# Half of the up products' low weight parts made by an adding transfer instead of VectorE

## The chip, the core and the metric

The kernel runs on one core of a Trainium2 chip. The time is the device time of one execution in microseconds; the median of three runs is given, and one more execution was recorded by the hardware profiler. TensorE (PE) multiplies, VectorE (DVE) and ScalarE (ACT) work on elements, GpSimd (POOL) does a few small things, and SyncE (SP) issues the transfers between DRAM and SBUF.

## What is computed

A network of two layers over 256 latent and 256 context positions, width 1024. Each layer is a feed-forward block, a token mixer (a gated linear recurrence, an mLSTM and windowed attention, merged by gates), and a second feed-forward block; all of them are normed, shifted and scaled by a condition. In the last layer the context is no longer needed after the mixer. The change touches the feed-forward blocks:

```
def swiglu(h, w1, w3, w2):
    return (jax.nn.silu(h @ w1) * (h @ w3)) @ w2

xl = xl + 0.5 * ml[:, :, 2] * swiglu(ln_mod(xl, norm_g[l, 0], ml[:, :, 0], ml[:, :, 1]),
                                     ffn_w1[l, 0], ffn_w3[l, 0], ffn_w2[l, 0])
```

`w1` and `w3` are 1024 x 2816, `w2` is 2816 x 1024, all in fp32.

## The kernel before

Latents and context lie side by side as 512 columns, with the width on the partitions in eight tiles `k`. A product is done with three matmuls for each `k` (`mm3`, L264 to L266), since PE works on rounded fp32 (`fp32r`): the high part of the weight by the high part of the input, the high part of the weight by the low part of the input, and the low part of the weight by the high part of the input. The inputs' parts are `hh` and `hl`, the weights' are `whi` and `wlo`.

The weights' parts are made on the chip. `raw_tile` loads 1024 KB of fp32 weights into one of three `raw` buffers (L235 or L240 in the profile, issued by SP). `split_w` then takes 512 columns at a time: ACT copies them to `whi`, which rounds them (L249), and DVE subtracts `whi` from them into `wlo` (L250). Each part takes a slot of SBUF from a list that is used in turn; in the feed-forward blocks 27 slots serve the weights, and while the condition's products run, one of them holds their scrap output `junk`.

The 2816 hidden columns are 22 chunks of 128, done in thirds of 8, 7 and 7. For each chunk, `load13` loads `w1` and `w3` (1024 columns each, so two halves of 512 for each product), `mm3` makes `p1` and `p3` with 2 x 8 x 3 matmuls, and `finish` puts them together (silu on ACT, L640, a product on DVE, L641, and the split into `gh` and `gl`, L283 and L284). After the chunks of a third come the down products `dn` of that third. The first three chunks of a block are made together, in tiles called `up`, while the norm is still being finished (`proj_first`). Tiles `p1` and `p3` both appear as `p` in the profile, where buffer numbers are left out.

There are four feed-forward blocks: (layer 0, first), (layer 0, second), (layer 1, first), and (layer 1, second), the last one over latents alone. In the first three, `filled` is true from the third chunk on: in these DVE also makes the condition's products for later norms (`junk` from `ada` tiles, L390), a few after each chunk, as far as `FEEDS` gives them.

The order of PE's instructions is that of the program. The other engines' instructions are put in order by the scheduler of the framework, from priorities and readiness. Each engine and each queue then runs strictly in its order. In the feed-forward blocks POOL runs the power that makes a norm's scale (`py`, L419), and some memsets of the mixer (`xp`, L763) come early on its queue.

Of the kernel before, what the change touches and what calls it, by code (L numbers as in the profile page):

```python
# [9 lines left out]
F32 = mybir.dt.float32  # L10
# [3 lines left out]
AF = mybir.ActivationFunctionType  # L14
ALU = mybir.AluOpType
# [69 lines left out]
def body(ctx, tc, ins, out):  # L85
    nc = tc.nc
# [9 lines left out]
    def nm(s):  # L96
        uid[0] += 1
        return f"{s}_{uid[0]}"
# [5 lines left out]
    def salloc(name, dt=F32, which=1):  # L104
        i = free[which].pop(0)
        t = sp.tile([P, SLOTW * 2 if dt == BF16 else SLOTW], dt, tag=f"slot{i}", name=nm(name))
        slot_of[id(t)] = (i, t, which)
        return t

    def sfree(*ts):  # L110
        for t in ts:
            i, _, which = slot_of.pop(id(t))
            free[which].append(i)
# [12 lines left out]
    def palloc(name, which=1):  # L126
        i = banks[which].pop(0)
        t = pp.tile([P, T], F32, tag=f"bank{i}", name=nm(name))
        bank_of[id(t)] = (i, t, which)
        return t  # L130

    def pfree(*ts):
        for t in ts:
            i, _, which = bank_of.pop(id(t))
            banks[which].append(i)
# [67 lines left out]
    V = nc.vector  # L203
    S = nc.scalar
# [25 lines left out]
    def raw_tile(src, n):  # L230
        r = wp.tile([P, 2048], F32, tag="raw", name=nm("raw"))
        if len(src.shape) == 3:
            nc.sync.dma_start(r[:, :n].rearrange("p (c f) -> p c f", c=src.shape[1]), src)
        else:
            nc.sync.dma_start(r[:, :n], src)  # L235
        return r
# [3 lines left out]
        nc.sync.dma_start(r, src)  # L240
        return r

    def split_w(r, n):

        w = []
        for a in range(0, n, 512):
            e = min(n - a, 512)
            hi, lo = salloc("whi", F32R, 0), salloc("wlo", F32R, 0)
            S.copy(hi[:, :e], r[:, a:a + e])  # L249
            V.tensor_tensor(lo[:, :e], r[:, a:a + e], hi[:, :e].bitcast(F32), op=ALU.subtract)  # L250
            w.append((hi, lo))
        return w

# [21 lines left out]
    def split_act(src, cols=BOTH, name="y"):  # L275

        hi = salloc(name + "h", F32R)
        lo = salloc(name + "l", F32R)
        split_into(hi, lo, src, cols)
        return hi, lo  # L280
# [44 lines left out]
    def ada_second():  # L325

        ps = palloc("ada")
        for k in range(KD):
            if k % 2 == 0:
                r = raw_tile(ins["ada1"][k // 2], 2 * D)  # L330
            for j in range(4):
                o = k % 2 * D + j * TL
                PE.matmul(ps[32 * j:32 * j + 32, 0:TL], cT[:, k, :], r[:, o:o + TL], start=(k == 0), stop=(k == KD - 1))
            if k % 2 and k < KD - 1:
                yield
        sb = salloc("adasb", which=2)
        S.copy(sb[:, 0:TL], ps[:, 0:TL])
        pfree(ps)

        def turn():  # L340
            ps2 = palloc("ada2")
            for q in range(2):
                PE.transpose(ps2[:, q * P:(q + 1) * P], sb[:, q * P:(q + 1) * P], ident)
            sfree(sb)
            b0 = V_ADAB + 32
            V.tensor_tensor(mods[0][:, 2].rearrange("p (j q) s -> p q j s", q=2),
                            ps2[:, 0:TL].rearrange("p (q j r) -> p q j r", q=2, j=4)[:, :, :, 0:2],
                            vec[:, 0, b0:b0 + 16].rearrange("p (j q s) -> p q j s", q=2, s=2), op=ALU.add)
            pfree(ps2)
            ada_done.add((0, 2))  # L350
        defer(2, turn)
# [188 lines left out]
    def lone_finish(p1, p3):  # L540

        c = small([P, 2], "shc")
        for i, p in enumerate((p1, p3)):
            V.tensor_copy(c[:, i:i + 1], p[:, TL:TL + 1])
        sl, t = salloc("silu", which=2), mp.tile([P, TL], F32, tag="xr", name=nm("xt"), bufs=3)
        V.tensor_tensor(sl[:, LAT], p1[:, LAT], rows[0][:, LAT], op=ALU.mult)
        S.activation(sl[:, LAT], sl[:, LAT], AF.Silu, bias=c[:, 0:1])
        V.tensor_tensor(t, p3[:, LAT], rows[0][:, LAT], op=ALU.mult)
        V.scalar_tensor_tensor(sl[:, LAT], t, c[:, 1:2], sl[:, LAT], op0=ALU.add, op1=ALU.mult)
        pfree(p1, p3)  # L550
        return sl
# [35 lines left out]
            wfree(w)  # L587


    def load13(l, j, m):  # L590
        r = raw_tile(ins["w13"][l, j, m], 2048)
        return [split_w(r[:, :1024], 1024), split_w(r[:, 1024:], 1024)]

    def passes_of(streams, load, use, ahead=None, begin=None):

# [27 lines left out]
    def ffn(l, j, streams, order, after, first, ahead, prep=None):  # L623

        n = 0 if j == 0 else 2
        both = len(streams) == 2
        cols = BOTH if both else LAT
        filled = False
        rate = FEEDS.get((l, j), 0) / 48
        second = ada_second() if l + j == 0 else None  # L630
        for ti, (a, b) in enumerate(THIRDS):
            kk = b - a
            gh, gl = [], []

            def finish(p1, p3, lone=False):
                if lone:
                    sl = lone_finish(p1, p3)
                else:
                    sl = salloc("silu", which=2)
                    S.activation(sl[:, cols], p1[:, cols], AF.Silu)  # L640
                    V.tensor_tensor(sl[:, cols], sl[:, cols], p3[:, cols], op=ALU.mult)  # L641
                    pfree(p1, p3)
                h, lo = split_act(sl, cols, "g")
                gh.append(h)
                gl.append(lo)
                sfree(sl)

            m = a
            if ti == 0:
                ps = [palloc("up", 0) for _ in first]  # L650
                if both:
                    proj_first(first, ps, order, prep)
                else:
                    lone_first(l, n, first, ps)
                for i in range(0, len(first), 2):
                    finish(ps[i], ps[i + 1], not both)
                if not both:
                    sfree(rows.pop(0))
                if j == 0 or l == 0:
                    cond_load()  # L660
                    filled = True
                m = a + len(first) // 2
            while m < b:
                w1, w3 = load13(l, j, m)
                p1, p3 = palloc("p1", 0), palloc("p3", 0)
                mm3(p1, w1, KD, hh, hl, cols)
                mm3(p3, w3, KD, hh, hl, cols)
                wfree(w1)
                wfree(w3)
                finish(p1, p3)  # L670
                if second:
                    next(second, None)
                if filled and m < b - 1:
                    feed(2 * rate)
                tick(2 * pe_us(cols, KD))
                m += 1
            if ti == 0:
                need((l, 3 * n + 2))
                gate_scale(l, n)

            def load2(np_):
                r = raw_tile(ins[f"w2_{ti}"][l, j, np_], 2 * kk * P)
                return [split_w(r[:, q * kk * P:(q + 1) * kk * P], kk * P) for q in range(2)]

            def down(s, o, w, ps=None):
                cc = cols if s is None else STREAMS[s]
                if ps is None:
                    ps = palloc("dn", 0)
                    mm3(ps, w, kk, gh, gl, cc)
                for s2 in streams if s is None else (s,):  # L690
                    x_add(l, n, o, ps, s2)
                    if ti == len(THIRDS) - 1:
                        after(s2, o)
                pfree(ps)
                if filled and s is None and ti < 2:
                    feed(rate)
                tick(pe_us(cc, kk))

            def down_first(ws):

                pss = [palloc("dn", 0) for _ in ws]
                for ks in (range(kk - 1), (kk - 1,)):
                    for ps, w in zip(pss, ws):
                        mm3(ps, w, kk, gh, gl, cols, ks)
                for o, (ps, w) in enumerate(zip(pss, ws)):
                    down(None, o, w, ps)

            if ti == len(THIRDS) - 1:
                passes_of(streams, load2, down, ahead, down_first)
            else:  # L710
                passes_of((None,), load2, down, None, down_first)
            if filled and ti == len(THIRDS) - 1:
                cond_free()
            sfree(*gh, *gl)
# [947 lines left out]
```

## Time and profile before

| what | value |
|---|---|
| median of 3 runs | 2201.46 us (2198.39 to 2201.73) |
| the profiled execution, its time | 2198.09 us |
| the profiled execution, its span | 2196.3 us |
| PE busy | 2160.1 us, 98% |
| DVE busy | 1440.5 us, 66% |
| ACT busy | 1026.0 us, 47% |
| POOL busy | 25.3 us, 1% |
| transfers | 310.26 MB, 40.1% of 16 engines' span |

The span runs from the first to the last instruction of the profile; the execution's time has a little around it. Busy times of engines overlap, so they don't add up to the span. The granted clock is the share of TensorE's full speed that the chip allowed: 0.999 over the span.

### The profile page before, as it was taken

The page shows a single profiled execution, that of the slowest core. Times are in us where ns is not written, and L with a number is a line of the kernel's source. Part 1 is how long each engine was busy: PE and PEld are TensorE (multiplying, and loading weights), DVE is VectorE, ACT ScalarE, POOL GpSimd, SP SyncE. Part 2 cuts the span into 40 slices and gives each one's busy share as a digit, 9 for nine tenths or more (in the row PEclk, how much of TensorE's full clock was granted, in tenths as well). Part 3 has the DMA queues.
Part 4 walks back from the last instruction along what each step waited for, and adds up shares of the span by engine and source line. Part 5 has one row for each costly group of instructions (what it writes and reads, how often), then busy time and mean ns, then how long its engine had stood idle before and what let it go on. Part 6 is the DMA issues. An engine that isn't in the chain of part 4 may idle for free.

```text
span 2196.3 us, 32299 instructions
## 1 busy us (share of the span) xinstructions
PE 2160.1 (98%) x12325; PEld 1840.8 (84%) x12325; DVE 1440.5 (66%) x3029; ACT 1026.0 (47%) x2031; POOL 25.3 (1%) x59
## 2 busy tenths in 40 slices
PE   6999999999999999999999999999999999999999
PEld 5778888977787778998888898888889778999999
DVE  5889634578776645699834378733345888868664
ACT  4322233468576534442232244232234778757553
POOL 0000000000000000000000000000000000000000
PEclk9999999999999999999999999999999999999999
DMA  9666422311122322366622237722222222454652
GB/s 362 240 245 227 161 91 101 112 60 61 67 69 77 125 87 96 135 212 225 228 96 110 89 107 273 242 101 94 91 99 95 68 89 92 152 188 169 232 191 96
DMA packets 73643, 310.26 MB, mean 141 GB/s; under 512 B 6928, under 2 KB 10512, under 8 KB 59024
## 3 DMA queue, kind: packets, MB, share of 16 engines
q1 hardware_dynamic: 73488, 308.19, 40.1%
q8 instruction: 97, 1.59, 0.3%
q14 instruction: 58, 0.48, 0.1%
HBM read 303.97 MB, written 4.19 MB: 140 GB/s over the span
## 4 chain that ended last, share of the span: by engine, by line
PE 89%; DVE 5%; ACT 4%; DMA 1%; issue 1%; POOL 0%; SPq 0%; ACTq 0%; DVEq 0%; POOLq 0%
PE p L264 11%; PE p L265 11%; PE p L266 11%; PE dn L264 6%; PE dn L265 6%; PE dn L266 6%; PE pg L264 3%; PE pg L265 3%; PE pg L266 3%; PE pj L264 2%; PE pj L265 2%; PE pj L266 2%; PE up L264 2%; PE up L266 2%; PE up L265 2%; PE pb L266 1%
## 5 line engine op out<-in xcount | busy, mean ns | idle before, releaser
L249 ACT CAST whi<-raw 128x512 fp32r<-128x512 f32 (+1 forms) x844 | 507.2, 612 | 824.3 <-PE p L265 371.4
L250 DVE TENSOR_TENSOR wlo<-raw,whi 128x512 fp32r<-128x512 f32 (+1 forms) x844 | 564.4, 678 | 415.1 <-ACT whi L249 337.8
L264 PE MATMUL p<-hh,whi 128*128 128x512 f32 (+1 forms) x1216 | 446.0, 367 | 0.0
L265 PE MATMUL p<-hl,whi 128*128 128x512 f32 (+1 forms) x1216 | 444.8, 366 | 0.0
L266 PE MATMUL p<-hh,wlo 128*128 128x512 f32 (+1 forms) x1216 | 444.7, 366 | 0.0
L390 DVE SCALAR_TENSOR_TENSOR junk<-ada,cb 128x1024 bf16<-128x1024 f32 x208 | 254.1, 1222 | 37.3 <-DMA ada<-ada 35.3
L264 PE MATMUL dn<-gh,whi 128*128 128x512 f32 (+1 forms) x809 | 275.7, 341 | 0.0
L266 PE MATMUL dn<-gh,wlo 128*128 128x512 f32 (+1 forms) x809 | 275.0, 340 | 0.0
L265 PE MATMUL dn<-gl,whi 128*128 128x512 f32 (+1 forms) x809 | 274.9, 340 | 0.0
L264 PEld LDWEIGHTS p<-hh,whi 128*128 128x128 f32 x1216 | 228.4, 188 | 41.9 <-issue 1.6
L266 PEld LDWEIGHTS p<-hh,wlo 128*128 128x128 f32 x1216 | 228.4, 188 | 41.4
L265 PEld LDWEIGHTS p<-hl,whi 128*128 128x128 f32 x1216 | 228.6, 188 | 40.1
L265 PEld LDWEIGHTS dn<-gl,whi 128*128 128x128 f32 x809 | 152.2, 188 | 18.8
L266 PEld LDWEIGHTS dn<-gh,wlo 128*128 128x128 f32 x809 | 152.1, 188 | 18.7
L264 PEld LDWEIGHTS dn<-gh,whi 128*128 128x128 f32 x809 | 152.1, 188 | 18.6
L264 PE MATMUL pj<-hh,whi 128*128 128x512 f32 (+1 forms) x400 | 154.2, 385 | 1.2 <-DVE li L842 1.2
L265 PE MATMUL pj<-hl,whi 128*128 128x512 f32 (+1 forms) x400 | 143.6, 359 | 0.0
L266 PE MATMUL pj<-hh,wlo 128*128 128x512 f32 (+1 forms) x400 | 143.3, 358 | 0.0
L264 PE MATMUL pg<-hh,whi 128*128 128x512 f32 (+1 forms) x384 | 130.2, 339 | 0.0
L265 PE MATMUL pg<-hl,whi 128*128 128x512 f32 (+1 forms) x384 | 129.6, 338 | 0.0
L266 PE MATMUL pg<-hh,wlo 128*128 128x512 f32 (+1 forms) x384 | 129.6, 338 | 0.0
L555 DVE SCALAR_TENSOR_TENSOR x<-dn,Ga,x 128x256 f32<-128x256 f32 x168 | 74.7, 479 | 53.0 <-PE dn L266 53.0
(291 smaller groups left out, 3363.0 us busy)
## 6 DMA issues: line engine op xcount, KB each, us to landing
raw<-w SPq DMA_DIRECT2D x104, 1024.0 KB, 4.9
ada<-ada SPq DMA_DIRECT2D x124, 512.0 KB, 4.0
raw<-win SPq DMA_DIRECT2D x30, 1024.0 KB, 4.9
raw<-w SPq DMA_DIRECT2D x32, 896.0 KB, 4.6
raw<-wbr SPq DMA_DIRECT2D x24, 1024.0 KB, 4.9
raw<-wbo SPq DMA_DIRECT2D x24, 512.0 KB, 3.6
raw<-wout SPq DMA_DIRECT2D x8, 1024.0 KB, 4.9
raw<-ada SPq DMA_DIRECT2D x6, 1024.0 KB, 6.4
```

Source lines behind the costliest of these rows:

```text
L249: S.copy(hi[:, :e], r[:, a:a + e])
L250: V.tensor_tensor(lo[:, :e], r[:, a:a + e], hi[:, :e].bitcast(F32), op=ALU.subtract)
L264: PE.matmul(o, hi[:, ws], xh[k][:, cols], start=(k == 0), stop=False)
L265: PE.matmul(o, hi[:, ws], xl[k][:, cols], start=False, stop=False)
L266: PE.matmul(o, lo[:, ws], xh[k][:, cols], start=False, stop=(k == kk - 1))
L390: V.scalar_tensor_tensor(junk[0][:, :D], r, 1.0, cb[0][:, s * D:(s + 1) * D], op0=ALU.mult, op1=ALU.mult, accum_out=am[:, b, s:s + 1])
L555: V.scalar_tensor_tensor(x[k][:, c], ps[:, c], Gate[l, n][:, k, s:s + 1], x[k][:, c], op0=ALU.mult, op1=ALU.add)
```

## The change

`split_w` gets the source in DRAM as a new argument. Where it is given, the second 512 columns of each product's weights take another way: ACT writes the negative of `whi` into `wlo`, and a transfer issued by POOL reads the same weights from DRAM once more and adds them onto `wlo`. The first 512 columns, and all other weights, go as before. `load13` passes the source only if it is told to, and the loop over chunks tells it so when `filled` is true: 19 chunks (3 to 21) in each of the first three feed-forward blocks. The first three chunks of a block are loaded without it.

```diff
-    def split_w(r, n):
+    def split_w(r, n, src=None):
         w = []
         for a in range(0, n, 512):
             e = min(n - a, 512)
             hi, lo = salloc("whi", F32R, 0), salloc("wlo", F32R, 0)
             S.copy(hi[:, :e], r[:, a:a + e])
-            V.tensor_tensor(lo[:, :e], r[:, a:a + e], hi[:, :e].bitcast(F32), op=ALU.subtract)
+            if src is not None and a:
+                S.activation(lo[:, :e], hi[:, :e].bitcast(F32), AF.Copy, scale=-1.0)
+                nc.gpsimd.dma_start(lo[:, :e], src[:, a:a + e], accum_op=ALU.add)
+            else:
+                V.tensor_tensor(lo[:, :e], r[:, a:a + e], hi[:, :e].bitcast(F32), op=ALU.subtract)
             w.append((hi, lo))
         return w
...
-    def load13(l, j, m):
-        r = raw_tile(ins["w13"][l, j, m], 2048)
-        return [split_w(r[:, :1024], 1024), split_w(r[:, 1024:], 1024)]
+    def load13(l, j, m, add=False):
+        src = ins["w13"][l, j, m]
+        r = raw_tile(src, 2048)
+        return [split_w(r[:, q * 1024:(q + 1) * 1024], 1024, src[:, q * 1024:(q + 1) * 1024] if add else None)
+                for q in range(2)]
...
             while m < b:
-                w1, w3 = load13(l, j, m)
+                w1, w3 = load13(l, j, m, filled)
```

## Rows read from the trace of the kernel before

**Rows 1.** The page: span, engines (busy us, share, instructions), the last chain by engine

```profile
span 2196.3 us, 32299 instructions
...
PE 2160.1 (98%) x12325; PEld 1840.8 (84%) x12325; DVE 1440.5 (66%) x3029; ACT 1026.0 (47%) x2031; POOL 25.3 (1%) x59
...
PE 89%; DVE 5%; ACT 4%; DMA 1%; issue 1%; POOL 0%; SPq 0%; ACTq 0%; DVEq 0%; POOLq 0%
```

**Rows 2.** Waits of PE: waiting line, releaser, total us, times, longest us

```profile
PE ada L304 <- DMA ada<-ada: 12.8, 1, 12.8
...
PE rot L1327 <- DVE p L950: 2.3, 2, 2.0
...
PE rgx L266 <- DVE wlo L250: 0.7, 2, 0.4
...
PE up L266 <- DVE wlo L250: 0.4, 1, 0.4
PE up L264 <- DVE x L555: 0.3, 1, 0.3
```

**Rows 3.** Stretches: length, PE, PEld, DVE, ACT, POOL busy, clock, DMA share, GB/s

```profile
66.00:128.00 62.00, 62.00 (x313) 47.54 (x312) 51.08 (x87) 20.19 (x37) 0.00 (x0) 1.00 0.76 274
...
289.00:367.00 78.00, 78.00 (x337) 62.97 (x336) 27.12 (x42) 23.96 (x41) 0.14 (x2) 1.00 0.27 89
961.00:1017.00 56.00, 56.00 (x245) 45.33 (x244) 54.44 (x93) 19.06 (x33) 0.00 (x0) 1.00 0.65 233
...
1333.00:1390.00 57.00, 57.00 (x248) 46.14 (x248) 43.46 (x76) 19.55 (x33) 0.00 (x0) 1.00 0.79 279
```

**Rows 4.** Timeline of ACT: start us, duration, what, idle before it and its releaser

```profile
200.45 0.59 ACT L640 ACTIVATE silu<-p 128x512 f32<-128x512 f32 x1
...
222.76 0.59 ACT L640 ACTIVATE silu<-p 128x512 f32<-128x512 f32 x1
...
262.70 0.62 ACT L249 CAST whi<-raw 128x512 fp32r<-128x512 f32 x1 [2.17 <-PE dn L265]
...
325.40 0.62 ACT L249 CAST whi<-raw 128x512 fp32r<-128x512 f32 x1 [1.28 <-PE p L265]
...
946.76 1.14 ACT L249 CAST whi<-raw 128x512 fp32r<-128x512 f32 x2 [0.15 <-PE up L265]
...
1319.13 1.14 ACT L249 CAST whi<-raw 128x512 fp32r<-128x512 f32 x2
```

**Rows 5.** Timeline of PE, matmuls that read a low part

```profile
292.34 0.40 PE L266 MATMUL p<-hh,wlo 128*128 128x512 f32 x1
...
359.35 0.40 PE L266 MATMUL p<-hh,wlo 128*128 128x512 f32 x1
...
1336.57 0.39 PE L266 MATMUL p<-hh,wlo 128*128 128x512 f32 x1
```

**Rows 6.** Groups by form: count, busy us, mean ns, idle before and releasers

```profile
L250 DVE TENSOR_TENSOR wlo<-raw,whi 128x512 fp32r<-128x512 f32 x780 | 528.8, 688 | 333.0 <-ACT whi L249 263.3 <-PE p L265 26.2 <-PE dn L265 12.4
L249 ACT CAST whi<-raw 128x512 fp32r<-128x512 f32 x780 | 474.5, 620 | 738.2 <-PE p L265 324.3 <-PE dn L265 186.9 <-PE pg L265 69.6
```

**Rows 7.** Issues of transfers: count, KB each, median us to landing

```profile
raw<-w SPq DMA_DIRECT2D x104, 1024.0 KB, 4.9
...
x<-xT SPq DMA_DIRECT2D x8, 256.0 KB, 5.5
xs<-x SPq DMA_DIRECT2D x8, 256.0 KB, 3.1
```

**Rows 8.** Timeline of POOL

```profile
289.08 0.10 POOL L763 MEMSET xp<- 128x4 f32 x1 [272.03 <-PE dn L265]
...
1303.95 1.66 POOL L419 TENSOR_TENSOR py<-msv,half 128x2 f32<-128x2 f32 x1 [15.88 <-DVE msv L471]
...
1550.58 0.10 POOL L763 MEMSET xp<- 128x4 f32 x1 [244.96 <-PE dn L265]
```

## Prediction, made before the result was known

> **What bounds the kernel now.** I read the shares of the engines first. TensorE (PE) is busy 98% of the span, VectorE (DVE) 66%, and 89% of the chain that ended last is PE work [rows 1]. A share over the whole span hides stages, so the waits of PE come next: one wait of 12.8 us before the first products, and then only small ones [rows 2]. Ten of the groups have a DVE instruction as the releaser; the largest is 2.3 us, the smallest 0.3 us, and together they are 11.9 us. Only two of them wait for a low weight part (`wlo`), 0.7 and 0.4 us, and both lie in the interleaved first products, which the change leaves as they are [rows 2]. The ones above them belong to the mixer.
>
> Then I looked at the stretches that the change touches, the loops over chunks of the up products. In four of them PE is busy for the whole stretch, whether DVE is at 35% (27.12 of 78.00 us) or at 97% (54.44 of 56.00 us), and whether the transfer engines are at 0.26 or at 0.79; the granted clock is 1.00, the upper level, throughout [rows 3]. A busy PE proves little where its ends are modelled, so I checked its pace. From one chunk's silu to the silu two chunks later it is 222.76 - 200.45 = 22.31 us, so 11.155 us a chunk [rows 4]. A chunk is 48 matmuls (two products, eight k, three terms), so 0.2324 us a matmul with nothing left between chunks. DVE at 97% therefore costs these loops nothing.
>
> Why not? A low part is made long before it is used. Weight halves live in 27 slots, of which one holds `junk` in these loops: 26 slots, 13 halves of two. A new half is cast when the oldest one is let go, and PE then has 12 halves in front of it, 12 x 12 x 0.2324 = 33.5 us. The trace agrees: a cast at 325.40 us ends its wait on PE's second term [rows 4], and the matmul that reads that half's low part begins at 359.35 us [rows 5]. From the cast's end (326.02) that is 33.3 us. The margin is smallest at chunk 3 of a stage, where the first six matrices still hold 24 slots. In the third stage touched, the second half of chunk 3 is cast from 1319.13, so until about 1319.75, and is read at 1336.57: 16.8 us [rows 4, 5]. In the second stage the cast of the same half waits for the first products and starts at 946.76 [rows 4].
>
> **The change part by part.** It runs for 19 chunks in each of three stages, 57 chunks, with two halves in each: 114 halves.
>
> Removed: 114 subtractions on DVE at 688 ns [rows 6], 78.4 us of 1440.5 us [rows 1], or 1.38 us of each chunk's 11.155 us. At the fullest stretch DVE goes from 97% to 85% [rows 3]. PE waits for none of it there, so on the path it is worth 0. Taking every DVE wait of PE in the whole kernel away would give 11.9 us; those in reach of this edit are the 0.4 us and 0.7 us ones at most [rows 2]. So the gain lies between 0 and 1.1 us; I take 0.
>
> Added on ScalarE (ACT): 114 copies with a sign. The trace has no such form; the nearest of the same size is the cast at 620 ns [rows 6]. With it that is 70.7 us, 1.24 us a chunk. ACT has 23.96 us of work in 78 us, 3.43 us a chunk [rows 3], and goes to 4.67 of 11.155. Queued behind each copy are the next cast, the silu and the cast of `gh`, each 0.6 us later. The cast has 16.8 us or more in hand, and the silu only frees one of three pairs of PSUM banks, a chunk each. On the path: 0. That cover would be gone if ACT came near 11.155 us a chunk.
>
> Added on the transfers: 114 of 128 x 512 fp32, 256 KB, issued by POOL. The trace has no accumulating transfer and none issued by POOL. From below, a plain 256 KB transfer lands after 3.1 us when quiet and 5.5 us in the crowded start [rows 7]. From above I have only the 1024 KB load with 4.9 us [rows 7], for a transfer that has to read its destination too and hence moves more than its 256 KB; doubling the crowded one gives 11 us. I take 6 us (between quiet and crowded, with some for the read of the destination and the issue) and keep 3.1 and 11. The chain for the tightest half is then 0.62 (copy) + 6 = 6.6 us, at the upper end 11.6 us, against 16.8 us: no wait on PE in either case, 0 us.
>
> By the Trainium skill, page "DMA: Bandwidth & Descriptors", section "Anatomy of one DMA — SWDGE (gpsimd) path", a POOL-issued transfer takes about 2.0 us plus its bytes over 436 GB/s; an estimate from that is 2.6 us, and the sum would stay 0. No row here shows it.
>
> Pace matters as well as delay: two transfers in 11.155 us, so each may hold the transfer engines for 5.58 us. In the first stretch 274 GB/s cost 0.76 of the engines, 0.0028 for each GB/s [rows 3]. The added 2 x 262,144 bytes in 11.155 us are 47 GB/s: 0.13 as plain traffic, 0.26 if the read of the destination counts as much again. The fullest stretch goes from 0.79 to 0.92, at worst to 1.05 [rows 3]; 0.05 of 57 us is 3 us of delay to loads that feed parts 16 us or more ahead. On the path: 0.
>
> Moved on the queues: SP issues nothing new; a raw buffer's last reader in these chunks becomes ACT's cast, so it comes free no later. POOL now carries 114 issues in order, each waiting for ACT's copy. Behind a waiting issue would stand POOL's power for the norms and the mixer's memsets [rows 8]. The powers of a norm come before PE can free the slot that the first issue waits for (1303.95 against the cast at 1319.13) [rows 4, 8], so no norm waits.
>
> The sum: 0 (DVE) + 0 (ACT) + 0 (transfers) + 0 (queues). The profiled execution was 2198.1 us with a span of 2196.3, 1.8 us around it; the median of the runs is 2201.5, 3.4 us above. The forecast is the median unchanged, 2201.5 us. About 0.2%, 4.4 us, is what a measurement of this kernel can tell from no change.
>
> **The rivals.**
>
> *The accumulating transfers are too slow (slower).* The place is the up loops; it decides above 5.58 us of the engines for one transfer. At 8.5 us, two of them take 17.0 us a chunk and fall 5.8 us behind. A third of five chunks collects 29 us, less 16 in hand is 13; each third of seven collects 41, less 32 is 9. So 31 us a stage, 93 us in three: about 2295 us. Just above the limit, at 7.5 us, the long thirds stay covered (7 x 3.85 = 27 us) and the short one loses 3: about 2211 us. For it: adding needs the destination read and written, and DVE runs beside it at up to 97%. Against it: a plain transfer of that size lands in 3.1 us [rows 7], so its hold must be more than twice that. I give it 0.11.
>
> The Trainium skill has a rule that would bring this about: page "SBUF — State Buffer", section "A bandwidth-pool intuition that's wrong (but worth ruling out)", says that a POOL-issued transfer can stand still behind a DVE instruction in a two-port mode, 620 ns becoming 3100 ns. Five times 3.1 us would be 15 us and this rival in full; but its section "Who interferes with whom" says that `tensor_tensor` has no such mode, and the long DVE work of these loops is of two-input kinds. No row here shows either.
>
> *POOL's queue is blocked (slower or the same).* The mixer's memset stands on POOL at 289.08 after a wait of 272.03 us for a slot, and again at 1550.58 [rows 8]. If it were placed ahead of the issues of chunks 15 to 17, those would wait till then. The second half of chunk 15 was cast from 262.70 and is read at 292.34 [rows 4, 5]; issued at 289.1 and landing after 3.1 to 11 us it would be 0 to 8 us late, at two places: 0 to 16 us, at 6 us twice 2.8, about 2207 us. Against it: the memset runs far ahead of its place in the program, so POOL is ordered by readiness, and the issues are ready 26 us earlier. Chance 0.06.
>
> *DVE's relief is worth something (faster).* If the lighter DVE let work behind the loops start sooner, up to the 11.9 us of PE's DVE waits could go [rows 2]: 2190 us, half of it 2195.5 us. Against it: most of these lie in the mixer, where nothing changes. Chance 0.06.
>
> *It is not done as said.* If POOL itself added the numbers instead of the transfer engines, POOL's busy time would jump, but PE would still have its 16 us: the same time, inside the forecast.
>
> **How the numbers follow.** Forecast (no wait on PE) 0.77, slow transfers 0.11, blocked POOL 0.06, faster 0.06. Half of the blocked case stays within 0.2%, and 0.01 of the forecast may drift out on the slow side: faster 0.06, same 0.79, slower 0.15. The range leaves out most of the faster case beyond half of its gain and the slow transfers beyond their beginning: 2195.5 to 2211 us.
>
> **What would show it.** Right: DVE's subtraction group of that shape falls from 780 to 666, its busy time by about 78 us; ACT gains a group of 114 near 0.6 us; PE's waits show no `p` with the transfer as releaser; a chunk still takes 11.16 us; the transfer share in the up loops rises by 0.13 to 0.26. Wrong: `p` at the third term waiting for `wlo`'s transfer (slow transfers), POOL issues bunched right after a memset (blocked queue), or ACT's table loads rising with the copies. The prediction would fail most cheaply if an accumulating transfer holds the engines for over 5.6 us.

## The result and the profile after

The changed kernel takes 2219.24 us (median of 4 runs, 2215.21 to 2220.68), the kernel before 2199.93 us in the same comparison. The ratio is 1.0087, with a 95% interval of 1.0074 to 1.0099: slower, by some 19 us. The forecast was 2201.5 us with no change, in a range up to 2211. Stages 1 to 3 are the three feed-forward blocks that the change touches.

The page of the changed kernel, with the lines that answer to [rows 1] and the share of the transfer queues:

```profile
span 2213.4 us, 32457 instructions
...
PE 2165.1 (98%) x12325; PEld 1842.6 (83%) x12325; DVE 1368.1 (62%) x2915; ACT 1087.2 (49%) x2145; POOL 124.2 (6%) x173
...
q1 hardware_dynamic: 73488, 308.19, 39.6%
q0 software_dynamic: 16416, 29.89, 8.4%
...
PE 76%; DVE 9%; DMA 8%; ACT 4%; issue 2%; POOL 0%; SPq 0%; DVEq 0%; ACTq 0%; POOLq 0%
```

DVE did lose its 72 us of work and PE's share still says 98%. But in the chain that ended last, DVE and the transfers went from 5% and 1% to 9% and 8%. PE's waits (columns as in [rows 2]) say where:

```profile
PE ada L309 <- DMA ada<-ada: 13.4, 3, 12.9
PE dn L269 <- ACT gh L288: 8.4, 4, 4.0
...
PE dn L270 <- DVE gl L289: 3.0, 3, 1.6
```

Two groups are new, 11.4 us together, and neither is a wait for a low weight part: the down products wait for their own input, `gh` and `gl`. To see which of them, I set the same matmul of both traces side by side, by its place in the program (the n-th `dn` of the one against the n-th of the other):

```
place                          start before   start after   later by
end of third 1, stage 1            137.42         139.17       1.75
end of third 2, stage 1            253.63         259.62       5.99
9 matmuls on                       255.95         264.35       8.40
13 matmuls on                      256.88         266.05       9.17
end of third 1, stage 2           1026.96        1039.15      12.19
end of third 1, stage 3           1399.09        1415.97      16.88
9 matmuls on                      1401.18        1419.70      18.52
end of the span                   2196.3         2213.4       17.1
```

(The end of a third is here the down matmul for which PE came to wait: the one that first reads the last chunk's `gl`, in third 2 of stage 1 the one that first reads `gh` of the last chunk but one.) The whole loss arises at four places: where a third ends whose chunks had `ada` tiles beside them. In the fifth such third, the second of stage 2, the tiles stop after two chunks, and there is no loss. Between the four places the two traces keep their distance, and behind the last it even shrinks a little. Here is one of the four, the end of the first third of stage 3. First PE and DVE before, then after, in timelines:

```profile
1389.10 0.39 PE L264 MATMUL dn<-gh,whi 128*128 128x512 f32 x1
```

```profile
1390.94 0.68 DVE L641 TENSOR_TENSOR silu<-silu,p 128x512 f32<-128x512 f32 x1
```

```profile
1401.42 0.39 PE L269 MATMUL dn<-gh,whi 128*128 128x512 f32 x1
...
1413.88 0.51 PE L269 MATMUL dn<-gh,whi 128*128 128x512 f32 x1 [2.54 <-ACT gh L288]
1415.97 0.52 PE L270 MATMUL dn<-gl,whi 128*128 128x512 f32 x1 [1.59 <-DVE gl L289]
```

```profile
1412.49 0.68 DVE L648 TENSOR_TENSOR silu<-silu,p 128x512 f32<-128x512 f32 x1
```

Before, DVE made the last chunk's silu product 1.84 us after PE turned to the down products; after, 11.07 us after. PE can fill that time only with the other seven k of the first two down matrices: 42 matmuls of 0.2324 us, 9.76 us. From the product's start to the end of `gh` it takes 1.3 us, so the margin is 8.5 us; 11.07 - 8.5 is 2.6 us, and the row shows 2.54.

DVE was late because it stood behind missing `ada` tiles. Its waits for them, before and after (columns as in [rows 2]):

```profile
DVE junk L390 <- DMA ada<-ada: 35.3, 32, 5.2
```

```profile
DVE junk L395 <- DMA ada<-ada: 99.7, 61, 4.8
```

The issues of transfers, one line of before and two of after (columns as in [rows 7]): the adding one lands in 5.7 us, and the tiles went from 4.0 to 4.9 us. These are medians over the whole program, counted from the start of the issue.

```profile
ada<-ada SPq DMA_DIRECT2D x124, 512.0 KB, 4.0
```

```profile
ada<-ada SPq DMA_DIRECT2D x124, 512.0 KB, 4.9
...
wlo<-w POOLq DMA_DIRECT2D x114, 256.0 KB, 5.7
```

The stretches of [rows 3] in the changed kernel, and three short ones at the second of the four places (columns as there; the eighth number is the granted clock):

```profile
66.00:128.00 62.00, 62.00 (x313) 47.53 (x311) 42.42 (x71) 23.26 (x43) 5.18 (x6) 1.00 0.85 283
...
289.00:367.00 78.00, 78.00 (x337) 63.01 (x336) 21.86 (x37) 30.09 (x51) 8.78 (x12) 1.00 0.50 132
...
961.00:1017.00 56.00, 56.00 (x282) 47.09 (x282) 44.47 (x78) 24.74 (x46) 6.96 (x8) 1.00 0.87 273
...
1333.00:1390.00 57.00, 57.00 (x300) 48.51 (x299) 35.00 (x60) 23.14 (x42) 8.76 (x10) 1.00 0.89 279
...
255.00:260.00 5.00, 1.03 (x4) 0.48 (x2) 4.88 (x9) 1.05 (x3) 0.00 (x0) 0.92 0.53 161
260.00:262.00 2.00, 2.00 (x5) 1.37 (x5) 1.93 (x5) 1.91 (x4) 0.00 (x0) 0.50 1.02 416
262.00:267.00 5.00, 5.00 (x15) 3.85 (x15) 2.49 (x5) 1.55 (x3) 0.00 (x0) 0.60 0.81 287
```

The transfer engines went from 0.76 to 0.85, from 0.65 to 0.87 and from 0.79 to 0.89 in the three stretches with tiles; the chunks themselves still leave PE no gap. These means hide a shorter stretch. The first 20 us of stage 3's loop, before and after (it starts 12 us later there):

```profile
1333.00:1353.00 20.00, 20.00 (x89) 16.23 (x89) 15.52 (x28) 7.67 (x14) 0.00 (x0) 1.00 0.82 292
```

```profile
1345.00:1365.00 20.00, 20.00 (x91) 16.28 (x90) 8.90 (x14) 6.39 (x11) 3.08 (x4) 1.00 1.02 330
```

Here the transfer engines are full by the profile, 1.02 against 0.82 before. In the table of stretches above, the last three lines show a second cost: after a wait of almost 4 us the clock is granted at 0.50, the lower level.

### The profile page after: what moved, and what is told of

Read it like the earlier page. It is cut to its first block, busy times and chain, and to the rows that moved or that the text cites. A ratio compares the mean times of both kernels' runs of the same rounds, so it can differ in the third digit from the quotient of the medians.

```text
span 2213.4 us, 32457 instructions
## 1 busy us (share of the span) xinstructions
PE 2165.1 (98%) x12325; PEld 1842.6 (83%) x12325; DVE 1368.1 (62%) x2915; ACT 1087.2 (49%) x2145; POOL 124.2 (6%) x173
## 3 DMA queue, kind: packets, MB, share of 16 engines
q1 hardware_dynamic: 73488, 308.19, 39.6%
q0 software_dynamic: 16416, 29.89, 8.4%
q8 instruction: 97, 1.59, 0.3%
## 4 chain that ended last, share of the span: by engine, by line
PE 76%; DVE 9%; DMA 8%; ACT 4%; issue 2%; POOL 0%; SPq 0%; DVEq 0%; ACTq 0%; POOLq 0%
PE p L269 9%; PE p L270 9%; PE p L271 8%; DMA ada<-ada 6%; PE dn L270 5%; PE dn L269 5%; PE dn L271 5%; PE pg L269 3%; PE pg L270 3%; PE pg L271 3%; DVE junk L395 2%; PE pj L269 2%; PE pj L270 2%; PE pj L271 2%; DVE wlo L255 2%
## 5 line engine op out<-in xcount | busy, mean ns | idle before, releaser
L255 DVE TENSOR_TENSOR wlo<-raw,whi 128x512 fp32r<-128x512 f32 (+1 forms) x730 | 486.3, 675 | 357.6 <-ACT whi L250 279.1
L288 ACT CAST gh<-silu 128x512 fp32r<-128x512 f32 (+1 forms) x88 | 49.9, 568 | 203.1 <-DVE silu L648 203.1
L253 POOL DMA_DIRECT2D wlo<-w x114 | 98.9, 887 | 816.0 <-ACT wlo L252 783.7
```

What stands on the lines that cost most here:

```text
L253: nc.gpsimd.dma_start(lo[:, :e], src[:, a:a + e], accum_op=ALU.add)
L288: S.copy(hi[:, cols], src[:, cols])
```

## The experiments

Theory A: the transfers hold up the `ada` tiles, DVE stands in order behind the missing tile, so the silu product of a third's last chunk comes too late for the down products. Theory B: ACT's extra copies, in order before silu and `gh`, are what comes late. Others are named where they are tested. All ratios are to the kernel before, on the same chip.

**1. No transfer, the copies stay.**

```diff
-                nc.gpsimd.dma_start(lo[:, :e], src[:, a:a + e], accum_op=ALU.add)
+                V.tensor_tensor(lo[:, :e], r[:, a:a + e], lo[:, :e].bitcast(F32), op=ALU.add)
```

> The adding transfer is replaced by an addition on DVE (weights plus the negative high part), so ACT's 114 copies stay, DVE has its 114 instructions back, and no byte is moved by POOL. Theory A (the transfers delay the landing of the condition's ada tiles, DVE stands in order behind the tile that is missing, and the silu product of a third's last chunk comes late): 2197 to 2204 us, DVE's wait for ada tiles 35 to 45 us, no dn wait of PE. Theory B (ACT's extra copies delay silu and gh): 2212 us or more, with PE's dn waits as in the changed kernel (11 us).

Measured: 2198.29 us, ratio 0.9999 (0.9989 to 1.0008), ada wait 31.3 us, no `dn` wait. The copies are there, in a group of their own (by form; columns as in [rows 6]):

```profile
L252 ACT ACTIVATE wlo<-whi 128x512 fp32r<-128x512 f32 x114 | 71.4, 632 | 3.0
```

71.4 us more on ACT cost nothing. Theory B falls.

**2. The transfer copies and doesn't add.**

```diff
-                nc.gpsimd.dma_start(lo[:, :e], src[:, a:a + e], accum_op=ALU.add)
+                nc.gpsimd.dma_start(lo[:, :e], src[:, a:a + e])
```

> The transfer copies the weights over the low part and doesn't add (the low parts of these halves are then wrong, so the output is); everything else as in the changed kernel. Theory A with adding as the cost: in the changed kernel POOL's queue takes 0.281% of the engines per MB and SP's 0.129%, 2.2 times as much; without the adding the extra share is less than half, so a loss of 3 to 10 us over before, 2203 to 2210 us, ada wait of DVE 50 to 80 us. Theory A with mere issue or traffic as the cost, and theory B: 2214 to 2221 us as in the changed kernel.

Measured: 2198.73 us, ratio 1.0001 (0.9992 to 1.0010). Less than expected: nothing at all is lost, although DVE waits 76.4 us for tiles, over twice the 35.3 us of before. The page's queues, the waits of DVE, and the end of stage 3's first third in timelines of DVE and PE:

```profile
q0 software_dynamic: 16416, 29.89, 5.4%
```

```profile
DVE junk L395 <- DMA ada<-ada: 76.4, 57, 5.4
```

```profile
1397.08 0.68 DVE L648 TENSOR_TENSOR silu<-silu,p 128x512 f32<-128x512 f32 x1
```

```profile
1400.50 0.49 PE L270 MATMUL dn<-gl,whi 128*128 128x512 f32 x1 [0.23 <-DVE gl L289]
```

The down products began at 1390.1 us here, so the product is 7.0 us behind them: DVE is late, but by less than the margin of 8.5 us. PE waits 0.23 us for `gl`. The price of a late product is a threshold. The other traces agree: over all these kernels, PE waits for `gh` at the end of a first third only where the last product starts more than 8.5 us behind PE's turn (none up to 8.53 us; 0.5 to 0.7 us at 9.2 to 9.3 us, 2.5 us at 11.07 us, 5.3 us at 14.07 us). For the same 29.89 MB the copying transfers take 5.4% of the engines and the adding ones 8.4%; that difference carries DVE over it.

This run also settles a rival. The scheduler gave DVE another order in the changed kernel than before, with other numbers of tile products between the silu products, and that order might by itself have made them late. But here all 2915 DVE instructions stand in the order of the changed kernel, and nothing is lost.

**3. Three ada buffers instead of two, and the control.** The one edit is made to the changed kernel, the same to the kernel before:

```diff
-NSLOT = 56
+NSLOT = 55
...
-NADA = 2
+NADA = 3
```

> The changed kernel with three ada buffers instead of two (one general slot less, to make room). Theory A (a round trip of two buffers is too long for the pace of the tiles once a landing takes about 5 us): most of the loss comes back, 2198 to 2206 us, DVE's wait for ada tiles under 50 us. Theory D (the transfer engines are full, so that more buffers don't help): 2212 us or more and the wait stays near 100 us. Theory B: 2212 us or more.

> Control for the run with three ada buffers: the kernel before with three of them and one general slot less. If the slot or the third buffer costs nothing by itself: 2196 to 2202 us, and the 11 us left in that run belong to the adding transfers. If the lost slot costs time: 2203 to 2209 us.

Measured: 2209.71 us, ratio 1.0048 (1.0031 to 1.0065), ada wait 44.3 us; the control 2204.08 us, ratio 1.0023 (1.0013 to 1.0034). The first lies between what A and the full engines were to give. The control explains a part: with three buffers and one slot less the kernel before itself loses 5.6 us. Against its control the change costs 2209.71 - 2204.08 = 5.6 us instead of 19. Of PE's `dn` waits 3.3 us are left, at the end of stage 3's first third alone, where the tiles are used fastest. So the third buffer takes most of the loss away, not all of it, and landing grows to 6.1 us with three in flight. In the first thirds of stages 1 and 2 the last product now starts 7.2 and 5.0 us behind PE's turn, inside the margin; in stage 3, where DVE's order now has 22 tile products in the five chunks of the loop instead of 19, it is 10.6 us, nearly what it was with two buffers (11.07).

**4. Adding only where tiles are streamed, and only where none are.** The thirds in question are the last of each stage and the second of stage 3 (no tiles), and all the others.

```diff
-                w1, w3 = load13(l, j, m, filled)
+                w1, w3 = load13(l, j, m, filled and not (ti == 2 or ((l, j) == (1, 0) and ti == 1)))
```

> The adding transfer only in the thirds in which ada tiles are streamed: 29 chunks of 57, 58 transfers. Theory A: the whole loss, 2213 to 2221 us. Theories by which each transfer or copy costs its share (ACT, POOL, PE's waits on semaphores): about half of the loss, 2207 to 2211 us.

> The adding transfer only in the thirds in which no ada tile is streamed (the last third of each stage, and the second of the third stage): 28 chunks, 56 transfers, the complement of the run before. Theory A (it hurts only by holding up ada tiles that DVE waits for): the time of before, 2196 to 2202 us, no dn wait of PE. If an adding transfer, its issue on POOL or its copy on ACT had a cost of its own: half of the loss, 2206 to 2211 us.

Measured: with tiles, 58 transfers, 2217.88 us, ratio 1.0086 (1.0071 to 1.0102), the whole loss. Without tiles (the condition without its `not`), 56 transfers, 2199.80 us, ratio 1.0005 (0.9996 to 1.0014), and no `dn` wait. An adding transfer, its issue on POOL and its copy on ACT cost nothing by themselves in these thirds.

**5. All transfers, no tiles to wait for.**

```diff
+        made = []
...
             if tiles:
-                loads.append(ada_tile(ins["ada"][tiles.pop(0)]))
+                src = ins["ada"][tiles.pop(0)]
+                if len(made) < NADA:
+                    made.append(ada_tile(src))
+                loads.append(made[len(tiles) % len(made)])
```

> The changed kernel with all 114 adding transfers, but the condition's products read the same two ada tiles again and again instead of loading new ones (118 loads of 512 KB are left out, the output is wrong). DVE does the same instructions and never waits for a tile. Theory A: 2195 to 2202 us, no dn wait of PE. If the adding transfers cost PE something by another way (late low parts, DVE slowed by POOL): 2210 us or more.

Measured: 2198.28 us, ratio 0.9994 (0.9985 to 1.0004). All 114 adding transfers are there (8.3% of the engines) and no `dn` wait. This run also takes 62 MB of traffic away, so alone it doesn't tell DVE's standing still from crowded engines; the next but one does.

**6. Twice as many.** `if src is not None and a:` becomes `if src is not None:`.

> Both halves of each product's weights by adding transfers: 228 instead of 114, and DVE has no subtraction left in these chunks. Theory A: DVE is further relieved but its tiles come still later, so the lateness at the fed thirds' ends grows from some 10 us to 15 to 22 us and PE waits that much more at each of three to four ends: 2230 to 2275 us. If DVE's own work were what makes the product late: 2199 to 2212 us, less than with half of them.

Measured: 2251.04 us, ratio 1.0238 (1.0223 to 1.0253): 53 us, nearly three times the loss, with DVE relieved of all its subtractions in these chunks. Its ada wait is 173.9 us. PE's waits:

```profile
PE dn L269 <- ACT gh L288: 20.3, 6, 6.1
...
PE p L271 <- DMA wlo<-w: 6.4, 3, 3.7
PE dn L270 <- DVE gl L289: 5.4, 5, 1.2
...
PE p L269 <- DVE silu L648: 2.9, 1, 2.9
```

Only here, at twice the number, does PE wait for a transferred low part at all.

**7. The tiles keep to the program's place.** Each ada load first waits for a mark that ACT sets after each chunk's `gh`, so that the stream can't run ahead of the chunks.

```diff
             if tiles:
-                loads.append(ada_tile(ins["ada"][tiles.pop(0)]))
+                src = ins["ada"][tiles.pop(0)]
+                r = wp.tile([P, D], F32, tag="ada", name=nm("ada"), bufs=NADA)
+                S.copy(r[:, 0:1], mark)
+                nc.sync.dma_start(r, src)
+                loads.append(r)
...
+    mark = cp.tile([P, 1], F32, name="mark")
+    nc.gpsimd.memset(mark, 0.0)
...
+                S.copy(mark, h[:, 0:1].bitcast(F32))
```

> The changed kernel, but each ada load waits for the chunk at which the program calls for it (ACT writes one column of the buffer from a mark that it sets after each chunk's gh, some 0.2 us an instruction, about 180 of them), so the stream is spread over all three thirds instead of running ahead in the first ones. Theory A: DVE is no longer behind at the ends of thirds, 2197 to 2206 us. If the lateness has nothing to do with the tiles running ahead: 2213 us or more.

Measured: 2198.07 us, ratio 0.9997 (0.9988 to 1.0007): all of the loss is gone, with 114 adding transfers at 8.3% of the engines and all the tiles. Waits of DVE, and the end of stage 3's first third in its timeline:

```profile
DVE junk L399 <- DMA ada<-ada: 196.9, 61, 6.4
```

```profile
1388.50 0.69 DVE L654 TENSOR_TENSOR silu<-silu,p 128x512 f32<-128x512 f32 x1 [1.66 <-PE p L271]
```

DVE waits for tiles twice as long as in the changed kernel, and no harm is done: at this end it has caught up, and waits for PE. So the sum of the waits is not the price. What counts is whether DVE is behind at the moment at which a third ends. The edit spreads both the loads and DVE's products of the tiles over all three thirds, and doesn't tell the one from the other.

**8. 228 transfers that only copy.** Experiments 2 and 6 together.

> 228 transfers by POOL that only copy (low parts of these chunks wrong). Theory A with the time on the transfer engines as what counts: they would take 10.8% of the engines' span, between the changed kernel's 8.4% and the 16% or so of 228 adding ones, so between 2215 and 2245 us, with dn waits of PE at the fed ends. If only an adding transfer can hold up the tiles: 2197 to 2205 us.

Measured: 2216.53 us, ratio 1.0079 (1.0064 to 1.0094), `dn` waits of 10.3 us, POOL's queue at 10.2% of the engines. Adding isn't needed for the loss; enough time on the engines does it too. The share alone doesn't order the runs exactly, though: 10.2% copying costs about as much as 8.4% adding.

No version was faster than the kernel before. Experiment 7 equals it, without a single `dn` wait of PE.

## Why the prediction was wrong

**What held.** That DVE's relief is worth nothing on the path: the subtraction group went from 780 to 666 and from 528.8 to 450.9 us, and PE got nothing for it. ACT's copies are 114 of 632 ns (I took 620) and hidden, by experiment 1. The transfer lands in 5.7 us (I took 6; the slowest took 11.8), and PE never waits for a transferred low part. POOL was not blocked: the memset of [rows 8] ran at 298.25 us, among the issues, with no harm. The added share of the engines was 0.09 to 0.23 in the four stretches (forecast 0.13 to 0.26). (The 0.26 that I read as the engines' lowest share before is 0.27 in [rows 3]; nothing rests on it.) The two groups after, by form:

```profile
L255 DVE TENSOR_TENSOR wlo<-raw,whi 128x512 fp32r<-128x512 f32 x666 | 450.9, 686 | 281.6 <-ACT whi L250 211.1 <-PE p L270 26.4 <-PE dn L270 15.6
L253 POOL DMA_DIRECT2D wlo<-w x114 | 98.9, 887 | 816.0 <-ACT wlo L252 783.7 <-DVE junk L395 18.9 <-ACT whi L250 8.7
```

**The step that failed** is the term of the transfers' pace: "3 us of delay to loads that feed parts 16 us or more ahead. On the path: 0." That is true of the weights, and I had followed only the weights. The other loads on the same engines are the `ada` tiles. They have two buffers, and DVE reads them in order, with the silu products queued behind. In the first third of stage 3 before, a tile landed 4.4 us after the start of its issue (median of 23, from the trace), and DVE used it for 1.22 us: 5.6 us for a buffer's round trip. SP issued four tiles in a chunk of 11.155 us there, two per buffer, one each 5.58 us. There was no slack to lose. SP's issues before:

```profile
1356.84 8.97 SPq L240 DMA_DIRECT2D ada<-ada x4
...
1367.86 8.65 SPq L240 DMA_DIRECT2D ada<-ada x4
```

The loss of slack came in a burst, and a mean over the stretch couldn't show it. After, POOL issued eight adding transfers from 1333.17 to 1356.40 us, about twice the two a chunk that I had reckoned with, and the engines were full. The six tiles issued from 1334 to 1358 us took 7.2 us to land (median; the longest 11.7); the nine issued in that part before took 4.5 us. DVE after, its waits for tiles and the first two silu products of the loop:

```profile
1345.90 1.22 DVE L395 SCALAR_TENSOR_TENSOR junk<-ada,cb 128x1024 bf16<-128x1024 f32 x1 [2.45 <-DMA ada<-ada]
...
1353.73 1.22 DVE L395 SCALAR_TENSOR_TENSOR junk<-ada,cb 128x1024 bf16<-128x1024 f32 x1 [4.79 <-DMA ada<-ada]
...
1362.77 1.22 DVE L395 SCALAR_TENSOR_TENSOR junk<-ada,cb 128x1024 bf16<-128x1024 f32 x1 [4.60 <-DMA ada<-ada]
...
1365.19 0.68 DVE L648 TENSOR_TENSOR silu<-silu,p 128x512 f32<-128x512 f32 x1
...
1379.29 0.68 DVE L648 TENSOR_TENSOR silu<-silu,p 128x512 f32<-128x512 f32 x1
```

These two products start 8.4 and 11.3 us behind PE's turn to the next chunk (1.2 and 1.1 us before). Behind the burst a tile lands in 4.45 us (median of 12; 4.35 us before), and DVE holds its pace: the last product of the third is still 11.07 us behind. With a round trip as long as the pace it doesn't catch up. In stage 2 DVE is 7.8 us behind at the first product already; in stage 1 the lateness grows step by step, from 1.8 us at the first product to 9.3 us at the end of the first third and 20.4 us in the second.

A second term stands with it: for ACT and DVE I wrote that the silu "only frees one of three pairs of PSUM banks, a chunk each". Inside a third that is so, and there the lateness indeed costs nothing. At its end the product feeds the down products, with a margin of 8.5 us (7.1 us in thirds of seven), not of a chunk or more. In third 2 of stage 1 DVE was two products late: that of the last chunk but one began at 258.23 us, 6.2 us after PE's turn to the down products at 252.00 us, and PE stood 3.97 us for it.

```profile
258.23 0.68 DVE L648 TENSOR_TENSOR silu<-silu,p 128x512 f32<-128x512 f32 x1
```

So none of my rivals was the one that came. The mechanism of the nearest, slow transfers, did not take place: an adding transfer held the engines for 1.6 us (8.4% of 2213.4 us over 114), well inside 5.58 us, and its waits on `p` are absent. The right rival would have been DVE standing behind tiles that land some us later while the engines are full.

**The sum after the fact.** By the table of places, the steps at the four ends come to about 13.5 us (1.1, 4.7, 3.0 and 4.7; 11.4 us of it are counted as waits), the slow clock behind two of them to 2.7 and 1.6 us, a later start to 0.7 us, and the part behind the last gives back 1.4 us: 17.1 us of span. That the tiles' landing is what holds DVE up is shown by DVE's waits above and by experiments 2, 4, 5 and 7 together. Why DVE's order lets the tiles run ahead into the first thirds is not shown. How the engines' time is shared between POOL's and SP's transfers stays open.

## What to carry to other kernels

When a change adds transfers, list every stream on the engines and work out each one's buffer round trip against its pace; the weights may be 30 us ahead while a two-buffer stream beside them has nothing in hand. Do it for the fullest 20 us, not for the mean of a stretch: here a mean of 0.89 held 20 us at 1.02, and a stream without slack carried the lateness of those 20 us to the end of the third. An engine that runs in order passes such a delay on to whatever stands behind the missing tile, and that costs time only where another engine's margin is small, most often where one stage hands over to the next. So read an engine's lateness at those places, not its busy share or the sum of its waits.

## What the runs showed of the hardware

After a wait of 3.97 us PE's clock was granted at 0.50 of full speed for 260 to 262 us and at 0.60 on average for the next 5 us, the lower of its two levels for most of that time. Matmuls began 0.43 us apart instead of 0.23, which cost 2.7 us on top of the wait:

```profile
259.62 0.80 PE L269 MATMUL dn<-gh,whi 128*128 128x512 f32 x1 [3.97 <-ACT gh L288]
...
261.36 0.63 PE L269 MATMUL dn<-gh,whi 128*128 128x512 f32 x1
261.79 0.63 PE L270 MATMUL dn<-gl,whi 128*128 128x512 f32 x1
```

After two waits of 2.54 and 1.59 us the clock was granted at 0.58 from 1416 to 1418 us and at 0.56 from 1418 to 1420 us, which cost 1.6 us. After waits of 1.39 and 1.19 us at the end of stage 2's first third it stayed at 1.00 (1037 to 1045 us):

```profile
1037.45 0.51 PE L269 MATMUL dn<-gh,whi 128*128 128x512 f32 x1 [1.39 <-ACT gh L288]
1039.15 0.50 PE L270 MATMUL dn<-gl,whi 128*128 128x512 f32 x1 [1.19 <-DVE gl L289]
```

A transfer of 256 KB from POOL took 0.89 us of POOL to issue, and per MB 0.28% of the engines' span when adding, 0.18% when copying (5.4% for 29.89 MB), against 0.13% for SP's loads (39.6% for 308.19 MB), which come in larger pieces.
